# Another order of the seven products of an output projection, and lo parts of eleven weight tiles formed by transfers that add

## The chip, the cores and the metric

The kernel runs on one core of one Trainium2 chip. The metric is the device time of one execution in microseconds. Before the change it is 800.76 us, the median of three runs (800.46 to 800.78).

## The reference: what is computed

One decoder layer on 512 tokens of width 1024, all in float32. Three mixers work side by side on the normalised input (attention in a sliding window with sinks, stick-breaking attention, attention to a memory of 256 entries); their outputs are gated, added, projected and normalised. A gated feed-forward network (FFN) of inner width 2816 follows:

```python
u = rms_norm(h, ln_mix_pre[l])
proj = jnp.einsum('bsd,de->bse', u, w_in[l])
...
merged = (g[:, :, 0] * jnp.einsum('bse,ed->bsd', y_swa, w_branch_swa[l])
          + g[:, :, 1] * jnp.einsum('bse,ed->bsd', y_sb, w_branch_sb[l])
          + g[:, :, 2] * jnp.einsum('bse,ed->bsd', y_mem, w_branch_mem[l]))
mix = jnp.einsum('bsd,de->bse', merged, w_out[l])
h = h + rms_norm(mix, ln_mix_post[l])
u = rms_norm(h, ln_ffn_pre[l])
a = jax.nn.silu(jnp.einsum('bsd,df->bsf', u, w_gate[l])) * jnp.einsum('bsd,df->bsf', u, w_up[l])
ffn = jnp.einsum('bsf,fd->bsd', a, w_down[l])
h = h + rms_norm(ffn, ln_ffn_post[l])
```

The change lies between `merged` and the first products with `w_gate` and `w_up`.

## The kernel before, in words

**Splitting.** TensorE multiplies rounded values (the type fp32r in the profile). To keep float32 accuracy each operand is split into hi, the rounded value, and lo, the rest. `split` does this with two instructions: ScalarE (ACT) casts raw to hi (L135), VectorE (DVE) subtracts hi from raw to get lo (L136). A product of two split operands takes three matmuls, hi with hi, lo with hi and hi with lo (`mm3`, L169, L171, L172). The second reads lo of the left operand, the tokens, the third lo of the right one, the weights.

**Seven products.** The larger matrix products are taken as 2 x 2 blocks with seven block products in place of eight, named p1 to p7. That needs sums of weight blocks and sums of token blocks. Sums of weights are made mostly by transfers: a plain load brings one block into SBUF (SyncE, called SP, issues it), and a transfer on the queue of GpSimd (POOL) adds another block from memory onto the same tile (`accum_op=ALU.add`). In the output projection that is `wo_raw` and `wo_plus` (L1034; tiles of 128x512, 256 KB), in the FFN `g_raw` (L1233) and `g_plus` (L1236; tiles of 128x1024, 512 KB). A tile that needs two or three additions gets them one after the other, each waiting for the landing of the one before. The blocks of p1, p2 and p4 of the FFN are plain blocks of the weights, and so are those of p2 and p3 of the output projection.

**Output projection.** `mix_mm(p, i)` is one block product for half i of the tokens: four k tiles times three matmuls of 512 columns, 12 matmuls, summed in a PSUM bank x, y or w. Products with the same bank add up in it: p1, p6, p7, p4 in x, p5, p3 in y, p2 in w. Between the products a join copies the state of a bank or combines it with an earlier copy: ACT after p1, p5 and p6, DVE after p2, p3 (mkp, L1113) and p7. A product may only add to its bank once the join has read the state before. `wo_split` makes hi and lo of the weight tiles.

**Normalising and turning.** `mix(t)` normalises 128 token rows (t from 0 to 3), adds the residual and normalises again for the FFN: two squares and the short steps of the inverse root on ACT (t_m, r_m), long products on DVE; it ends in the tile mt. Tiles 0 and 1 are ready after p3 of half 0 and half 1, tiles 2 and 3 after p4 of half 0 and half 1. `turn(t)` transposes the rows of a tile on TensorE (L1177, eight transposes of 128x128 into two PSUM banks `ut`), and `place` splits them into the left operands of the FFN: B11 and B21 from tiles 0 and 1 (casts at L1165), T1 and others from tiles 2 and 3.

**FFN.** The object `fs` of class `Stream` holds a list of units, each one weight tile of 128x1024 with its 24 matmuls of 256 columns. The list begins

```python
seq = [("p1", 0), ("p2", 0), ("p1", 1), ("p1", 2), ("p2", 1), ("p2", 2)]
seq += [("p5", 0), ("p6", 0), ("p5", 1), ("p3", 0), ("p6", 1), ("p7", 0), ("p3", 1), ("p7", 1), ("p4", 0)]
```

with (product, chunk). The text counts units from 0, so unit 1 is p2 of chunk 0, unit 2 p1 of chunk 1 and unit 3 p1 of chunk 2. In the profile p1 sums in gx, p2 in gw, later ones in gy. `fs.ahead(l, s)` issues the loads up to unit l and the splits up to unit s; `load_at(i, ...)` hangs further loads and additions on unit i: the plain loads for p5, p6 and p3 of chunk 0 on unit 2, their six additions on unit 3 (one for p5, two for p6, three for p3), the tile "t" for p7 of chunk 0 with its addition on unit 4.

**What sets the order.** A scheduler puts the instructions on the engines' queues largely as the program writes them, with pieces under `tc.high_priority()` pulled forward. Each engine then works its queue strictly in order: an instruction that waits holds up all behind it, and that holds for the transfers that SP and POOL issue too. `first.close()` ends the life of a pool of tiles (`wp`), and the pool `fp` of the FFN tiles takes its memory. The `hi`, `lo` and `raw` tiles of `fp` so wait for the last reader of the old ones, which is p3 of half 1, for its weights lie in `wp`.

The change lies between 380 and 490 us of 798. The functions that it touches and what calls them:

Of the kernel before, what the change touches and what calls it, by code (L numbers as in the profile page):

```python
# [32 lines left out]
class Stream:  # L33
# [24 lines left out]
    def ahead(self, load_to, split_to):  # L58
        while self.loaded <= min(load_to, len(self.units) - 1):
            u = self.units[self.loaded]  # L60
            for fn in u["load"]:
                fn()
            u["raw"] = u["src"]() if callable(u["src"]) else self.load(u["src"], u["n"])
            self.loaded += 1
        while self.have <= min(split_to, len(self.units) - 1):
            u = self.units[self.have]
            for fn in u["split"]:
                fn()
            u["hl"] = self.split(u["raw"], u["n"])
            self.have += 1  # L70

    def later(self, us, fn):
# [31 lines left out]
def tile_kernel(ctx, tc, a):  # L104
# [27 lines left out]
    def split(raw, hi, lo, sign=1.0):  # L132

        if sign == 1.0:
            ins = nc.scalar.copy(hi, raw)  # L135
            lows = nc.vector.tensor_tensor(lo, raw, hi.bitcast(F32), op=ALU.subtract)  # L136
        else:
            ins = nc.scalar.mul(hi, raw, sign)
            lows = nc.vector.scalar_tensor_tensor(lo, raw, sign, hi.bitcast(F32), op0=ALU.mult, op1=ALU.subtract)
        if "behind" in st:  # L140
            after(ins, st["behind"][0])
            after(lows, st["behind"][1])
        return ins

    uid = [0]

# [889 lines left out]
    def wo_split(p, key, k):  # L1036
        if p not in ("p6", "p3"):
            hl = tuple(ck(f"wo{p}{x}{k}", F32R)[:, :] for x in "hl")
        else:
            if k % 2 == 0:  # L1040
                uid[0] += 1
                st["wo_two"] = [wp.tile([P, 1024], F32R, tag=x, name=f"{x}{uid[0]}", bufs=4) for x in ("hi", "lo")]
            hl = tuple(x[:, (k % 2) * 512 : (k % 2) * 512 + 512] for x in st["wo_two"])
        split(wsum[key][k][:, :], *hl)
        wt[(p, k)] = hl

    def rstd_small(name, ss):
# [37 lines left out]
    def turned_d(k):  # L1085
        split(merged[k][:, 256:], *(x[:, 256:] for x in mrd[k]))
# [3 lines left out]
    def mix_mm(p, i):  # L1090
        if p in ("p1", "p5", "p2"):
            mbank[(MIX[p], i)] = aps(f"m{MIX[p]}{i}")
        ps = mbank[(MIX[p], i)]
        for k in range(4):
            if p == "p1":
                x, o = ma[k // 2], (k % 2) * 256
            else:
                x, o = {"p2": (mbd, 0), "p4": (mbd, 256), "p5": (mqs, 256), "p3": (mqs, 0), "p6": (mrd, 0), "p7": (mrd, 256)}[p]
                x = x[k]
            mm3(ps[:, :], cols(x, o + i * P, P), wt[(p, k)], k == 0 and p in ("p1", "p5", "p2"), k == 3)  # L1100
        with tc.high_priority():
            if p in ("p1", "p5", "p6"):
                t = mkeep[(p, i)] = ck(f"mk{p}{i}")
                nc.scalar.copy(t[:, :], ps[:, :])
            elif p == "p2":
                t = mkeep[("p1", i)]
                nc.vector.tensor_tensor(t[:, :], ps[:, :], t[:, :], op=ALU.add)
            elif p == "p3":
                t = mkeep[("p6", i)]
                nc.vector.tensor_tensor(t[:, :], ps[:, :], t[:, :], op=ALU.subtract)  # L1110
            elif p == "p7":
                t = mkeep[("p5", i)]
                nc.vector.tensor_tensor(t[:, :], t[:, :], ps[:, :], op=ALU.subtract)  # L1113

    def mix(t):
        xr = hres[t]
        i = t % 2
        ps = (mkeep[("p1", i)], mkeep[("p6", i)]) if t < 2 else (mbank[("x", i)], mkeep[("p5", i)])
        ss, ss2 = small(f"ssm{t}", 2), small(f"ssh{t}", 2)
        tmp = [ck(f"mt{t}{h}") for h in range(2)]  # L1120
        for h in (1, 0):
            nc.scalar.activation(tmp[h][:, :], ps[h][:, :], AF.Square, accum_out=ss[:, h : h + 1])
        for h in (1, 0):
            nc.vector.tensor_tensor(tmp[h][:, :], ps[h][:, :], gpost[h][:, :], op=ALU.mult)
        r = rstd_small(f"m{t}", ss)
        for h in range(2):
            nc.vector.scalar_tensor_tensor(xr[h][:, :], tmp[h][:, :], r, xr[h][:, :], op0=ALU.mult, op1=ALU.add)
            nc.scalar.activation(tmp[h][:, :], xr[h][:, :], AF.Square, accum_out=ss2[:, h : h + 1])
        r2 = rstd_small(f"h{t}", ss2)
        for h in range(2):  # L1130
            st["mixed"] = nc.vector.scalar_tensor_tensor(
                tmp[h][:, :], xr[h][:, :], r2, gfpre[h][:, :], op0=ALU.mult, op1=ALU.mult
            )
        return tmp
# [38 lines left out]
    def turn(t, tmp):  # L1173
        pt = [aps(f"ut{t}{h}") for h in range(2)]
        for h in range(2):
            for k in range(4):
                nc.tensor.transpose(pt[h][:, k * P : (k + 1) * P], tmp[h][:, k * P : (k + 1) * P], ident[:, :])  # L1177
        turned[t] = pt
        if t < 2:
            turned[t] = [ck(f"ur{t}{h}") for h in range(2)]  # L1180
            for h in range(2):
                place(("B11", "B21")[h], t, pt[h])
                nc.scalar.copy(turned[t][h][:, :], pt[h][:, :])
            return
        t1 = ck(f"t1{t}")
        nc.vector.tensor_tensor(t1[:, :], pt[0][:, :], turned[t - 2][0][:, :], op=ALU.subtract)
        st[("t1", t)] = t1
        return place("T1", t, t1)
# [38 lines left out]
    def g_src(n, i, j):  # L1227
        return a["w_gu"][:, n + i * HF, j].rearrange("p g k n -> p (g k n)")
# [285 lines left out]
    for k in range(4):  # L1514
        wo_split("p7", "b", k)
        turned_d(k)
    mix_mm("p3", 0)
    table("natural_log_exp_and_others")
    tmp[0] = mix(0)
    for k in range(4):  # L1520
        wo_split("p4", "r", k)
    for p in ("p5", "p6", "p3"):
        mix_mm(p, 1)
    first.close()
    fp = ctx.enter_context(tc.tile_pool(name="fp", bufs=9, reuse_waits="tile"))

    def f_split(raw, n):
        uid[0] += 1
        hi = fp.tile([P, 1024], F32R, tag="hi", name=f"hi{uid[0]}", bufs=4)
        lo = fp.tile([P, 1024], F32R, tag="lo", name=f"lo{uid[0]}", bufs=4)  # L1530
        if isinstance(raw, list):
            for i, x in enumerate(raw):
                split(x[:, :], hi[:, i * 512 : (i + 1) * 512], lo[:, i * 512 : (i + 1) * 512])
        else:
            split(raw[:, :n], hi[:, :n], lo[:, :n])
        return hi, lo

    fs = Stream(None, f_split, LOAD_AHEAD + 1)
# [43 lines left out]
        with tc.high_priority():  # L1582
            tmp[t] = mix(t)

    fs.ahead(2, -1)
    mixed(1)
    mix_mm("p7", 0)
    turn(0, tmp[0])
    mix_mm("p4", 0)
    mixed(2)  # L1590
    fs.ahead(4, 1)
    mix_mm("p7", 1)
    mix_mm("p4", 1)
    turn(1, tmp[1])
    mixed(3)
# [116 lines left out]
```

## Time and profile before

| | |
|---|---|
| median of three runs | 800.76 us (800.46 to 800.78) |
| the profiled execution | 800.18 us |
| its span, first to last instruction | 798.4 us |
| mean granted TensorE clock | 0.995 |
| instructions in the span | 12825 |
| chain that ended last | PE 93%, DVE 4%, ACT 1%, issue 1% |
| transfers | 120.70 MB, mean 151 GB/s |
| POOL's additions of FFN tiles (L1236) | 27 of 512 KB, median 7.4 us to landing |
| SP's plain loads of FFN tiles | 57 of 512 KB, median 5.6 us to landing |

Times in the profile are counted from the first instruction of the span. PE is TensorE's matmul, PEld its loading of weights, SPq the queue of SP. Of a group of instructions the profile gives line, engine, operation, and the tiles it writes and reads (out<-in); "x4" is a count, and three durations such as 603/618/632 are the shortest, the median and the longest in ns. In a list of waits "PE mx L169 <- DVE t_m L1055: 0.9, 1, 0.9" says that matmuls of line 169 into mx waited 0.9 us in all, once, at most 0.9, until DVE's instruction for t_m ended. In a timeline the columns are start, duration, engine, line, operation and tiles; brackets at the end hold the idle time before it and what ended it, and a row with x3 stands for three instructions in a run. A PE row's duration is longer than the distance to the next start, since matmuls are pipelined. In a list of transfers the last number is the us from issue to landing, a median where there are several.

### The profile page before, as it was taken

What the parts mean: (1) busy time and instruction counts of PE and PEld (TensorE: products, weight loads), DVE (VectorE), ACT (ScalarE), POOL (GpSimd) and SP (SyncE); (2) the same over time, 40 slices, a digit from 0 to 9 for tenths busy, and PEclk for the clock granted to TensorE, in tenths of its full rate; (3) what the DMA queues carried; (4) which work ended last, traced back from release to release, by engine and by line L of the source; (5) the groups of instructions that cost most, each with busy time, mean ns of one, the idle gap of its engine ahead of it and who ended that gap; (6) DMA issues with size and microseconds to landing.
All of it is one profiled execution on the core that took longest, in us unless ns stands there. A gap on an engine that the chain in (4) does not pass through costs nothing.

```text
span 798.4 us, 12825 instructions
## 1 busy us (share of the span) xinstructions
PE 782.0 (98%) x4851; PEld 694.0 (87%) x4851; DVE 637.1 (80%) x1010; ACT 467.7 (59%) x868; POOL 94.0 (12%) x119
## 2 busy tenths in 40 slices
PE   9999999999999999999999889999999999999996
PEld 6899887877878899899887689999999999888885
DVE  6998976854778795986798889967677767898797
ACT  6566755644654555666655767545444444666573
POOL 0102100000000001000161120100100000205200
PEclk9999999999999999999999999999999999999998
DMA  8443356122243208238675897987777752859802
GB/s 302 134 149 106 118 166 205 53 82 76 80 102 79 59 27 238 52 88 258 183 137 154 252 222 195 280 230 201 184 182 182 187 157 67 197 126 225 205 0 106
DMA packets 44750, 120.70 MB, mean 151 GB/s; under 512 B 4976, under 2 KB 6912, under 8 KB 44688
## 3 DMA queue, kind: packets, MB, share of 16 engines
q1 hardware_dynamic: 32448, 86.66, 33.3%
q0 software_dynamic: 11952, 33.02, 22.6%
q8 instruction: 38, 0.62, 0.3%
q14 instruction: 24, 0.20, 0.1%
q10 hardware_dynamic: 288, 0.20, 0.1%
HBM read 116.19 MB, written 3.67 MB: 150 GB/s over the span
## 4 chain that ended last, share of the span: by engine, by line
PE 93%; DVE 4%; ACT 1%; issue 1%; DVEq 0%; ACTq 0%
PE gx L169 5%; PE gx L172 5%; PE gx L171 5%; PE g L169 3%; PE g L172 3%; PE br L169 3%; PE br L171 3%; PE g L171 3%; PE br L172 3%; PE gy L169 3%; PE gy L172 3%; PE gy L171 3%; PE x L172 3%; PE x L169 3%; PE x L171 2%; PE qx L169 1%
## 5 line engine op out<-in xcount | busy, mean ns | idle before, releaser
L135 ACT CAST hi<-gw 128x1024 fp32r<-128x1024 f32 x77 | 80.0, 1048 | 76.6 <-DVE gw L1254 36.0
L136 DVE TENSOR_TENSOR lo<-gw,hi 128x1024 fp32r<-128x1024 f32 x77 | 93.5, 1222 | 34.0 <-ACT hi L135 34.0
L135 ACT CAST hi<-raw 128x1024 fp32r<-128x1024 f32 (+2 forms) x52 | 53.8, 1040 | 51.0 <-PE g L171 13.8
L136 DVE TENSOR_TENSOR lo<-raw,hi 128x1024 fp32r<-128x1024 f32 (+2 forms) x52 | 62.8, 1213 | 18.0 <-ACT hi L135 17.8
L1236 POOL DMA_DIRECT2D gw<-in_w_gu x27 | 23.3, 900 | 191.7 <-DMA gw<-in_w_gu 112.4
L135 ACT CAST hi<-r 128x1024 fp32r<-128x1024 f32 (+1 forms) x24 | 23.6, 982 | 19.1 <-PE y L172 5.3
L171 PE MATMUL x<-lo,lh 128*128 128x512 f32 x88 | 34.2, 389 | 0.0
L169 PE MATMUL x<-hi,lh 128*128 128x512 f32 x88 | 34.2, 389 | 0.0
L172 PE MATMUL x<-hi,ll 128*128 128x512 f32 x88 | 34.1, 389 | 0.0
L832 DVE TENSOR_TENSOR_SCAN p<-r,anew 128x512 f32<-128x512 f32 (+1 forms) x24 | 24.7, 1040 | 8.1 <-ACT r L189 7.6
L136 DVE TENSOR_TENSOR lo<-r,hi 128x1024 fp32r<-128x1024 f32 (+1 forms) x24 | 27.1, 1130 | 3.1 <-ACT hi L135 3.1
L136 DVE TENSOR_TENSOR lo<-qw,hi 128x1024 fp32r<-128x1024 f32 x18 | 22.0, 1220 | 8.1 <-ACT hi L135 8.1
L135 ACT CAST hi<-qw 128x1024 fp32r<-128x1024 f32 x18 | 18.9, 1050 | 16.1 <-PE g L171 3.7
L136 DVE TENSOR_TENSOR lo<-bp,hi 128x512 fp32r<-128x512 f32 x33 | 22.7, 720 | 6.3 <-ACT hi L135 6.2
L135 ACT CAST hi<-bp 128x512 fp32r<-128x512 f32 x33 | 19.1, 619 | 13.6 <-DMA bp<-in_w_dn 5.2
L169 PE MATMUL gw<-B21h,hi 128*128 128x256 f32 x88 | 25.4, 289 | 0.8 <-ACT B21h L1165 0.8
L172 PE MATMUL gy<-T1h,lo 128*128 128x256 f32 x88 | 25.0, 284 | 0.8 <-DVE lo L136 0.8
L169 PE MATMUL gx<-B11h,hi 128*128 128x256 f32 x88 | 25.4, 289 | 0.0
L172 PE MATMUL gw<-B21h,lo 128*128 128x256 f32 x88 | 25.3, 287 | 0.0
L171 PE MATMUL gx<-B11l,hi 128*128 128x256 f32 x88 | 25.2, 286 | 0.0
L172 PE MATMUL gx<-B11h,lo 128*128 128x256 f32 x88 | 25.2, 286 | 0.0
L171 PE MATMUL gw<-B21l,hi 128*128 128x256 f32 x88 | 25.2, 286 | 0.0
(1020 smaller groups left out, 2946.8 us busy)
## 6 DMA issues: line engine op xcount, KB each, us to landing
gw<-in_w_gu SPq DMA_DIRECT2D x57, 512.0 KB, 5.6
gw<-in_w_gu POOLq DMA_DIRECT2D x27, 512.0 KB, 7.4
raw<-in_w_p SPq DMA_DIRECT2D x26, 512.0 KB, 4.0
qw<-in_w_p SPq DMA_DIRECT2D x15, 512.0 KB, 4.0
raw<-in_w_br SPq DMA_DIRECT2D x12, 512.0 KB, 3.7
bp<-in_w_dn SPq DMA_DIRECT2D x22, 256.0 KB, 8.4
r<-in_w_dn POOLq DMA_DIRECT2D x10, 512.0 KB, 8.4
qw<-in_w_p POOLq DMA_DIRECT2D x6, 512.0 KB, 7.8
```

Of the source, the lines that this page charges most:

```text
L135: ins = nc.scalar.copy(hi, raw)
L136: lows = nc.vector.tensor_tensor(lo, raw, hi.bitcast(F32), op=ALU.subtract)
L169: one = nc.tensor.matmul(out, lh, rh, start=start, stop=False, skip_group_check=True)
L171: nc.tensor.matmul(out, *two, start=False, stop=False, skip_group_check=True)
L172: st["product"] = nc.tensor.matmul(out, *three, start=False, stop=stop, skip_group_check=True)
L832: ins = nc.vector.tensor_tensor_scan(p[:, :w], left1[i][:, :w], anew[:, o : o + w], 0.0, op0=ALU.mult, op1=ALU.max)
L1236: nc.gpsimd.dma_start(gw[(n, key)][:, :], g_src(n, i, j), accum_op=ALU.add)
```

## The change

**Lo by a transfer.** A new function `split_dma` takes the place of `split` for eleven plain weight tiles. ACT casts raw to hi as before, then ACT writes minus hi into lo, and POOL issues a transfer that adds the same block from memory once more onto lo. DVE's subtraction falls away. Eight of the tiles belong to p2 and p3 of the output projection, three are FFN units 1, 2 and 3.

**Order of the products.** From p7's splits on the program goes, with the half in brackets: p5(1), p3(0), mix(0) now at high priority, p6(1), p7(0), p3(1), end of the pool, mixed(1), loads to unit 3 with the split of unit 0, p4(0), mixed(2), p7(1), turn(0), loads to unit 4 with the splits of units 1 to 3, p4(1), turn(1), mixed(3). Before it was p3(0), mix(0), p5(1), p6(1), p3(1), end of the pool, loads to unit 2, mixed(1), p7(0), turn(0), p4(0), mixed(2), loads to unit 4 with the splits of units 0 and 1, p7(1), p4(1), turn(1), mixed(3), then the splits of units 2 and 3.

```diff
-            u["hl"] = self.split(u["raw"], u["n"])
+            u["hl"] = u.get("way", self.split)(u["raw"], u["n"])
...
+    def split_dma(raw, hi, lo, src):
+
+        nc.scalar.copy(hi, raw)
+        nc.scalar.mul(lo, hi.bitcast(F32), -1.0)
+        nc.gpsimd.dma_start(lo, src, accum_op=ALU.add)
...
-        split(wsum[key][k][:, :], *hl)
+        if p in ("p2", "p3"):
+            j, h = (1, 0) if p == "p2" else (1, 1)
+            split_dma(wsum[key][k][:, :], *hl, a["w_out"][:, h, 4 * j + k])
+        else:
+            split(wsum[key][k][:, :], *hl)
...
+    mix_mm("p5", 1)
     mix_mm("p3", 0)
     table("natural_log_exp_and_others")
-    tmp[0] = mix(0)
+    with tc.high_priority():
+        tmp[0] = mix(0)
     for k in range(4):
         wo_split("p4", "r", k)
-    for p in ("p5", "p6", "p3"):
-        mix_mm(p, 1)
+    for p, i in (("p6", 1), ("p7", 0), ("p3", 1)):
+        mix_mm(p, i)
     first.close()
...
+    def f_split_dma(raw, src):
+        uid[0] += 1
+        hi = fp.tile([P, 1024], F32R, tag="hi", name=f"hi{uid[0]}", bufs=4)
+        lo = fp.tile([P, 1024], F32R, tag="lo", name=f"lo{uid[0]}", bufs=4)
+        split_dma(raw[:, :], hi[:, :], lo[:, :], src)
         return hi, lo
...
-    fs.ahead(2, -1)
     mixed(1)
-    mix_mm("p7", 0)
-    turn(0, tmp[0])
+    for i, (p, n) in enumerate(seq[:4]):
+        if i > 0:
+            fs.units[i]["way"] = lambda raw, w, n=n, j=(0 if p == "p1" else 1): f_split_dma(raw, g_src(n, 0, j))
+    fs.ahead(3, 0)
     mix_mm("p4", 0)
     mixed(2)
-    fs.ahead(4, 1)
     mix_mm("p7", 1)
+    turn(0, tmp[0])
+    fs.ahead(4, 3)
     mix_mm("p4", 1)
     turn(1, tmp[1])
     mixed(3)
```

The rows that follow are the engines' queues around the change. A name ends in the tile's number, which differs between the two kernels; in brackets stand the semaphores that an instruction waits for (DMAHW are landings of plain loads, DMASW landings of POOL's transfers). The lines of `mm3` are 169, 171 and 172 before and 175, 177 and 178 now.

TensorE at the end of p7 of half 0 (wop7, wop4 and hi/lo are weights of p7, p4 and p3, mx and my the banks), before:

```order
L172 MATMUL mx_4418<-wop7h_4607,mrl_4483 128x512
L169 MATMUL mx_4418<-wop4h_4661,mbd4h 128x512 [waits DVE_49,Activation_49]
L171 MATMUL mx_4418<-wop4l_4662,mbd4h 128x512
L172 MATMUL mx_4418<-wop4h_4661,mbd4l 128x512
L169 MATMUL my_4677<-hi_4318,mqh_4448 128x512 [waits Activation_49]
```

and now:

```order
L178 MATMUL mx_4426<-wop7h_4615,mrl_4491 128x512
L175 MATMUL my_4621<-hi_4322,mqh_4456 128x512 [waits Activation_49]
L177 MATMUL my_4621<-lo_4323,mqh_4456 128x512
...
L178 MATMUL my_4621<-hi_4347,mql_4469 128x512
L175 MATMUL mx_4426<-wop4h_4684,mbd4h 128x512 [waits DVE_49,Activation_49]
```

Where p4 of half 0, which waits for the join after p7, stood directly behind p7 with three of its matmuls ahead of p3 of half 1, all 12 matmuls of p3 of half 1 now stand between the two.

POOL's queue behind the additions of the output projection; gw are raw FFN tiles (4728, 4730 and 4732 those of p5, p6 and p3 of chunk 0, 4859 that of p7 of chunk 0, 4862 one of chunk 1), before:

```order
L1236 DMA gw_4728<-in_w_gu 128x1024 [waits DMAHW1_49,PE_49]
L1236 DMA gw_4730<-in_w_gu 128x1024 [waits DMAHW2_49,DMASW7_49,PE_49]
L1236 DMA gw_4732<-in_w_gu 128x1024 [waits DMAHW3_49,DMASW0_49,PE_49]
L1236 DMA gw_4730<-in_w_gu 128x1024 [waits DMASW7_49,DMASW1_49]
L1236 DMA gw_4732<-in_w_gu 128x1024 [waits DMASW2_49,DMASW0_49]
L1236 DMA gw_4859<-in_w_gu 128x1024 [waits DMAHW6_49,DMASW3_49]
L1236 DMA gw_4862<-in_w_gu 128x1024 [waits DMAHW7_49,DMASW4_49]
L1236 DMA gw_4732<-in_w_gu 128x1024 [waits DMASW5_49,DMASW2_49]
```

and now, where 4783, 4785, 4787, 4884 and 4887 are the same five in the same order, and lo_4892, lo_4897 and lo_4902 belong to units 1, 2 and 3:

```order
L1246 DMA gw_4783<-in_w_gu 128x1024 [waits DMAHW1_49,PE_49]
L149 DMA lo_4892<-in_w_gu 128x1024 [waits DMASW7_49,Activation_49]
L1246 DMA gw_4785<-in_w_gu 128x1024 [waits DMAHW2_49,DMASW0_49,PE_49]
L1246 DMA gw_4787<-in_w_gu 128x1024 [waits DMAHW3_49,DMASW1_49,PE_49]
L1246 DMA gw_4785<-in_w_gu 128x1024 [waits DMASW2_49,DMASW0_49]
L1246 DMA gw_4884<-in_w_gu 128x1024 [waits DMAHW6_49,DMASW3_49]
L1246 DMA gw_4787<-in_w_gu 128x1024 [waits DMASW4_49,DMASW1_49]
L149 DMA lo_4897<-in_w_gu 128x1024 [waits DMASW5_49,Activation_49]
L149 DMA lo_4902<-in_w_gu 128x1024 [waits DMASW6_49,Activation_49]
L1246 DMA gw_4787<-in_w_gu 128x1024 [waits DMASW7_49,DMASW4_49]
L1246 DMA gw_4887<-in_w_gu 128x1024 [waits DMAHW7_49]
```

The transfer for lo of unit 1 stands second, and those for units 2 and 3 stand eighth and ninth, behind the second additions to 4785 and 4787; on TensorE the third matmul of unit 2 (gx from B11h_3613 and lo_4897) now waits for that transfer.

ACT where it places the first turned rows (ut_4899 and ut_4900 are tile 1 turned, hi_4957 and hi_4961 units 2 and 3), before:

```order
L1165 CAST B11h_3613<-ut_4899 128x2x128 [waits PE_49]
L135 CAST hi_4957<-gw_4734 128x1024 [waits DMAHW4_49]
L1165 CAST B21h_3617<-ut_4900 128x2x128 [waits PE_49]
L189 ACTIVATE t_m_4827<-ssm_4817,b_m_4825 128x1 [waits DVE_49,Activation_49]
L135 CAST hi_4961<-gw_4857 128x1024 [waits DMAHW5_49]
L189 ACTIVATE r_m_4828<-t_m_4827 128x1 [waits Activation_49]
L1165 CAST B11h_3615<-ut_4899 128x2x128 [waits DVE_49]
L1165 CAST B21h_3619<-ut_4900 128x2x128 [waits DVE_49]
```

and now (ut_4862 is tile 0, ut_4918 tile 1, hi_4896/lo_4897 and hi_4901/lo_4902 units 2 and 3; the last row shown is the second quarter of tile 1):

```order
L1175 CAST B11h_3613<-ut_4918 128x2x128 [waits PE_49]
L147 CAST hi_4896<-gw_4789 128x1024 [waits DMAHW4_49]
...
L148 ACTIVATE lo_4897<-hi_4896 128x1024 [waits Activation_49]
...
L1175 CAST B11h_3615<-ut_4862 128x2x128 [waits DVE_49]
L147 CAST hi_4901<-gw_4797 128x1024 [waits DMAHW5_49]
L1193 COPY ur_4872<-ut_4862 128x512 [waits DVE_49]
L1138 ACTIVATE mt_4817,ssh_4816<-xr_4504 128x512 [waits DVE_49]
L1138 ACTIVATE mt_4818,ssh_4816<-xr_4505 128x512 [waits DVE_49]
L1175 CAST B21h_3617<-ut_4863 128x2x128
...
L148 ACTIVATE lo_4902<-hi_4901 128x1024
...
L1175 CAST B11h_3615<-ut_4918 128x2x128
```

Between the first and the second cast of tile 1 into B11 there now lie the rest of tile 0's casts, two casts and two multiplications of 128x1024, a copy, and two squares for the normalisation.

More of the change, by code (lines that the diff above doesn't have):

```diff
@@ L1535, in f_split @@
             split(raw[:, :n], hi[:, :n], lo[:, :n])
+        return hi, lo
+    def f_split_dma(raw, src):
[3 more added lines that the diff above has]
+        split_dma(raw[:, :], hi[:, :], lo[:, :], src)
         return hi, lo
```

## The prediction, made before the changed kernel had run

> **What bounds the kernel now.** I read the page first, then the waits, the table of windows, and the timelines of TensorE and of POOL between 430 and 490 us, where the change lies. Every line number in this part is that of the kernel before.
>
> ```profile
> PE 782.0 (98%) x4851; PEld 694.0 (87%) x4851; DVE 637.1 (80%) x1010; ACT 467.7 (59%) x868; POOL 94.0 (12%) x119
> ```
>
> TensorE is busy for 98% of the span, so a thing costs or gains time only where TensorE stands still. The windows say where that is (columns: length, then busy us of PE, PEld, DVE, ACT, POOL, granted PE clock, DMA share, GB/s):
>
> ```profile
> 410.00:420.00 10.00, 10.00 (x46) 8.27 (x45) 10.00 (x23) 6.67 (x17) 3.89 (x4) 1.00 0.70 149
> 430.00:440.00 10.00, 9.13 (x41) 7.27 (x40) 7.58 (x16) 5.25 (x14) 0.00 (x0) 1.00 0.03 6
> 440.00:450.00 10.00, 9.22 (x44) 6.98 (x43) 8.43 (x20) 7.04 (x18) 1.44 (x2) 1.00 0.66 243
> 450.00:460.00 10.00, 6.97 (x36) 5.79 (x35) 9.38 (x24) 8.53 (x23) 1.14 (x2) 0.83 1.04 282
> 460.00:470.00 10.00, 7.74 (x64) 7.30 (x62) 8.15 (x22) 6.46 (x20) 3.49 (x4) 1.00 1.03 244
> ```
>
> Up to 437 us TensorE is full. In 430 to 470 it is idle for 0.87 + 0.78 + 3.03 + 2.26 = 6.9 us, and in 450 to 470 the DMA engines are full (1.04, 1.03). The waits of TensorE name the causes:
>
> ```profile
> PE ut L1177 <- DVE mt L1131: 4.5, 3, 2.2
> PE mx L169 <- DVE t_m L1055: 0.9, 1, 0.9
> PE gw L169 <- ACT B21h L1165: 0.8, 1, 0.8
> PE mx L169 <- DVE mkp L1113: 0.8, 1, 0.8
> PE gy L172 <- DVE lo L136: 0.8, 1, 0.8
> PE gy L169 <- ACT hi L135: 0.2, 1, 0.2
> ```
>
> Two waits for joins of the output projection (mx, 0.9 and 0.8), three for the normalised rows that the transposes read (ut, 4.5 in all), and little else. No wait for a transfer is among them. POOL's own timeline shows transfers that are slow all the same, with nobody on TensorE behind them:
>
> ```profile
> 448.10 0.86 POOL L1236 DMA_DIRECT2D gw<-in_w_gu  x1 [23.57 <-DMA gw<-in_w_gu]
> 449.42 0.86 POOL L1236 DMA_DIRECT2D gw<-in_w_gu  x1 [0.46 <-issue]
> 450.70 0.86 POOL L1236 DMA_DIRECT2D gw<-in_w_gu  x1 [0.42 <-issue]
> 462.73 0.86 POOL L1236 DMA_DIRECT2D gw<-in_w_gu  x1 [11.17 <-DMA gw<-in_w_gu]
> 466.29 2.63 POOL L1236 DMA_DIRECT2D gw<-in_w_gu  x3 [2.70 <-DMA gw<-in_w_gu]
> 472.03 0.86 POOL L1236 DMA_DIRECT2D gw<-in_w_gu  x1 [3.11 <-DMA gw<-in_w_gu]
> ```
>
> These are the transfers that add, onto the raw tiles of FFN products p5, p6 and p3. The fourth stands 11.17 us in the queue until the landing of an earlier one, since a second addition to the same tile waits for the first. The list of issues in three windows, each around one of the first three and then the fourth and the last, gives their times to landing:
>
> ```profile
> gw<-in_w_gu POOLq DMA_DIRECT2D x1, 512.0 KB, 10.3
> gw<-in_w_gu POOLq DMA_DIRECT2D x1, 512.0 KB, 12.8
> gw<-in_w_gu POOLq DMA_DIRECT2D x1, 512.0 KB, 15.3
> gw<-in_w_gu POOLq DMA_DIRECT2D x1, 512.0 KB, 6.5
> gw<-in_w_gu POOLq DMA_DIRECT2D x1, 512.0 KB, 9.2
> ```
>
> So they land at 448.10 + 10.3 = 458.4, 462.2, 466.0, 469.2 and 481.2 us. While plain loads run beside them they land 3.8 us apart. After that they are alone: the five from 466.0 to 481.2 (fourth to eighth) lie 15.2/5 = 3.04 us apart, the shortest known step being 472.0 - 469.2 = 2.8, the longest 3.2.
>
> **The change, part by part.** First, the order of the products. Before, p4 of half 0 comes right behind p7 of half 0 and waits for its join:
>
> ```profile
> 437.43 0.39 PE L172 MATMUL mx<-wop7h,mrl 128*128 128x512 f32 x1
> 438.69 0.47 PE L169 MATMUL mx<-wop4h,mbd4h 128*128 128x512 f32 x1 [0.87 <-DVE t_m L1055]
> 439.46 0.40 PE L169 MATMUL my<-hi,mqh 128*128 128x512 f32 x1
> ```
>
> Now p3 of half 1 stands between, 12 matmuls at the 0.227 us that starts lie apart in a product (438.69 would have been 437.66). p3 of half 1 so starts at 437.66 rather than 439.46: 1.8 us earlier. The second wait for a join (0.8) gets the 8 transposes of rows 0 to 127 as cover. Both are gone: worth 1.03 + 0.8, and with p3's join 1.8 earlier, the normalisation of tile 1 comes up to 1.8 us earlier to its 2.2 us wait. That would be 3.6 us, if nothing later held TensorE.
>
> What else hangs on p3 of half 1 are the loads of the FFN weights. The queue of SP says so, and when they go out:
>
> ```profile
> SPq L1233 <- PE my L172: 20.9, 1, 20.9
> 442.41 2.97 SPq L1233 DMA_DIRECT2D gw<-in_w_gu  x6
> ```
>
> They start 1.8 us earlier too: 440.6.
>
> Second, the eight w_out tiles of p2 and p3. DVE loses eight subtractions of 0.68, ACT gets eight multiplications, for which the row shows the casts of the same size (0.62 us), POOL eight issues of 0.9 us:
>
> ```profile
> L136 DVE TENSOR_TENSOR lo<-wob,hi x4: 677/679/1487, 401.6 to 407.2; 128x512 fp32r<-128x512 f32 x4
> L135 ACT CAST wop2h<-wob x4: 603/618/632, 387.4 to 395.5; 128x512 fp32r<-128x512 f32 x4
> L1034 POOL DMA_DIRECT2D wor<-in_w_out x12: 850/858/1193, 374.2 to 423.7; - x12
> DMA to landing us min/median/max: 4.3/7.1/9.2
> ```
>
> The last cast for p2 is at 395.5; two ACT steps, seven issues ahead of the last one on POOL (7 x 0.9) and the longest landing (9.2) make 412.3, and the first of those tiles is read at about 416, that of p3 at about 430. TensorE has no gap there to gain. I cost this part at nothing; its cover is four microseconds, and past it each microsecond is one.
>
> Third, the three FFN tiles: the lo parts of units 1, 2 and 3 (p2 of chunk 0, p1 of chunks 1 and 2). This decides. On DVE one took 1.22 us:
>
> ```profile
> L136 DVE TENSOR_TENSOR lo<-gw,hi 128x1024 fp32r<-128x1024 f32 x77 | 93.5, 1222 | 34.0 <-ACT hi L135 34.0
> L135 ACT CAST hi<-gw 128x1024 fp32r<-128x1024 f32 x77 | 80.0, 1048 | 76.6 <-DVE gw L1254 36.0
> ```
>
> Now it is 1.05 on ACT (a multiplication of the size of that cast) and a 512 KB addition on POOL's queue, in the window with the full DMA engines. By the order of POOL shown ahead, lo of unit 1 stands second, but those of units 2 and 3 stand eighth and ninth: behind the second additions to gw_4785 and gw_4787, each of which waits for the first to land. That is where 11.17 and 2.70 us were waited before. And TensorE reads lo of unit 2 with the third matmul of that unit, which before ran at
>
> ```profile
> 466.10 0.29 PE L172 MATMUL gx<-B11h,lo 128*128 128x256 f32 x1
> 470.05 1.23 PE L1177 MATMUL ut<-c_ident,mt 128*128 128x128 f32 x8 [1.15 <-DVE mt L1131]
> ```
>
> The sum. The first group of additions now has four in it (gw_4783, lo of unit 1, gw_4785, gw_4787) and ended before at 466.0 with three. It starts 1.8 earlier and is one addition longer: 466.0 - 1.8 + 3.0 = 467.2. Only then POOL can issue the second addition to gw_4787 and, 0.86 later, lo of unit 2 (468.2 or so). In the queue of transfers that one is fourth after 467.2 (the second addition to gw_4785, gw_4884, the second to gw_4787, lo): 467.2 + 4 x 3.04 = 479.4 us. Lo of unit 3 lands at 482.4. Against 466.10 the third matmul of unit 2 comes 13.4 us later, at 479.5.
>
> Ahead of that TensorE has nothing else to do for about ten microseconds, and its clock will drop. Before, after the idle stretch that began at 452, matmuls with 256 columns started 0.21 apart and not 0.12:
>
> ```profile
> 458.28 0.41 PE L172 MATMUL gw<-B21h,lo 128*128 128x256 f32 x1
> 458.50 0.41 PE L169 MATMUL gw<-B21h,hi 128*128 128x256 f32 x1
> 466.34 0.28 PE L171 MATMUL gx<-B11l,hi 128*128 128x256 f32 x1
> 466.46 0.28 PE L172 MATMUL gx<-B11h,lo 128*128 128x256 f32 x1
> ```
>
> The clock of 0.83 over 10 us is 3.4 us at half. So 16 matmuls at 0.212 and the remaining six at 0.12, together 4.1 us instead of 2.64, and the transposes of tile 3 start at 483.6, where they started at 470.05 (their own wait of 1.15 is then long over): 13.5 us later. Lo of unit 3 is there by its third matmul at about 485. Two later waits, 0.8 and 0.2 for gy, fall away, since DVE and ACT get ahead meanwhile: 12.5 us remain. What the first part gains is swallowed, since it lies ahead of a wait for a transfer. The profiled execution took 800.18 us around its span of 798.4, and the median is 800.76, 0.58 above it: 810.9 for the span, 812.7 for such an execution, **813.3** for the median.
>
> Bounds: if the added addition fits into gaps and the steps are 2.8, lo of unit 2 lands at 464.2 + 11.2 = 475.4, and with a full clock 7.1 us remain: 807.9. If it costs 3.8, the steps are 3.2, all 22 matmuls run slowly and no later wait falls away, it is 468.0 + 12.8 = 480.8 and 15.5 us: 816.3. I take the middle steps, as they come from five transfers of this very queue and size.
>
> The rows above have 6.5 to 15.3 us from issue to landing. The Trainium skill ("DMA: Bandwidth & Descriptors", the section "Anatomy of one DMA — SWDGE (gpsimd) path") fits such a transfer as 2.0 us plus its bytes over 436e3. My estimate from that page for 524288 bytes is 3.2 us, and by it no addition would wait long for another and lo of unit 2 would be there before 460: by that rule the second rival below would happen. The trace disagrees in all five rows, since the engines are full.
>
> **The rivals.** *The transfers are in time, but turning is late.* The second additions would have to be issued before 458. Then TensorE waits for the turned rows: between the casts of tile 1's first quarter (about 452) and of its second (B11h_3615), ACT now has four steps of 1.05, two squares, a copy and small ones, some 8 us, with DVE's two products for tile 2 (0.7 each) behind them, against 3.4 us from first to last cast before. Unit 0 goes on at about 462.8, and the transposes of tile 3 come at about 472.2, 2.1 late, less the 1.0: 801.9. For it speaks that DVE has three long steps less; against it the 11.17 us.
>
> *Faster: the cover works.* The mechanism is the first part alone: joins hidden (1.03 + 0.8), tile 1 earlier (1.8). 800.76 - 3.6 = 797.2. It decides only if lo of unit 2 lands before 466 and the casts of turned rows keep their old places; for it speak the waits of TensorE quoted first, against it both orders.
>
> *The w_out additions are late as well.* Sixteen additions of 256 KB, at half of 3.04 each, take 24 us from 389 to 413 on DMA engines that were at 0.70 in 410 to 420 already. If ACT stands in its order behind a cast of a tile not landed, mbd7h comes after 416 and p2 waits; at 3 us: 816.3.
>
> **How the numbers follow.** The queue as computed: 0.78. Late w_out additions on top: 0.08. In time with late turning: 0.08. Faster: 0.06. The likeliest case alone is 807.9 to 816.3; I stretch it to **805 to 817**, since a landing some microseconds earlier is the easiest miss, and leave the two cases below 803 outside. About 0.2% (1.6 us) can be told from no change: faster 0.06, same 0.05 (most of the late turning), slower 0.89.
>
> **What would show it.** A wait of TensorE for a transfer into lo, 8 to 11 us, at the third matmul of p1 of chunk 1, with a PE clock below 1 after it; POOL issuing that transfer only at about 468, behind a long wait for gw; no more waits for t_m or mkp, and loads from about 440.6. I am wrong if lo of unit 2 is issued before 460 or lands less than 6 us after issue, or if TensorE stops ahead of 437.

## The result: 1.7% slower

| | before | changed |
|---|---|---|
| median | 800.72 us (800.46 to 800.78, 4 runs) | 813.97 us (813.38 to 814.44, 4 runs) |
| ratio | | 1.0166 (95% interval 1.0148 to 1.0183) |
| profiled execution, span | 800.18, 798.4 us | 813.38, 811.6 us |
| mean granted TensorE clock | 0.995 | 0.984 |

813.3 us was forecast, 805 to 817 the range. First the page of the changed kernel, busy time and chain:

```profile
PE 784.5 (97%) x4851; PEld 697.1 (86%) x4851; DVE 630.6 (78%) x999; ACT 474.9 (59%) x879; POOL 103.4 (13%) x130
PE 90%; DVE 3%; issue 3%; DMA 2%; POOL 1%; ACT 0%; SPq 0%; DVEq 0%; POOLq 0%; ACTq 0%
```

Transfers and POOL, which had no share in the chain that ended last, have one now. The waits of TensorE say which:

```profile
PE gx L178 <- DMA lo<-in_w_gu: 10.7, 1, 10.7
PE gx L175 <- ACT B11h L1175: 3.9, 1, 3.9
PE ut L1187 <- DVE mt L1141: 2.6, 2, 1.3
PE mw L175 <- ACT mbd7h L135: 0.7, 1, 0.7
```

One wait of 10.7 us for a transfer into lo, where no wait for a transfer was before. The two waits for joins (mx) are gone, and those for ut are 2.6 in place of 4.5 us. Two larger waits are new beside it: 3.9 us for the second quarter of the turned rows, and 0.7 us in p2 of the output projection, far ahead of the rest. The same stretches as before the change:

```profile
410.00:420.00 10.00, 9.13 (x40) 6.93 (x39) 8.67 (x17) 5.12 (x10) 6.68 (x6) 1.00 1.06 205
430.00:440.00 10.00, 10.00 (x46) 8.29 (x45) 7.87 (x17) 7.40 (x18) 0.00 (x0) 1.00 0.03 6
440.00:450.00 10.00, 10.00 (x49) 8.23 (x48) 9.16 (x22) 6.64 (x15) 1.50 (x3) 1.00 0.63 229
450.00:460.00 10.00, 5.04 (x23) 3.84 (x21) 7.38 (x22) 9.34 (x26) 2.02 (x3) 0.76 1.05 296
470.00:480.00 10.00, 0.00 (x0) 0.00 (x0) 5.45 (x12) 4.90 (x10) 3.94 (x5) 0.61 1.06 205
480.00:490.00 10.00, 9.38 (x59) 9.38 (x60) 3.19 (x5) 2.62 (x5) 0.12 (x1) 0.71 0.69 135
```

Between 430 and 450 TensorE is now full, so the covers work. From 470 to 480 it does nothing at all, while the DMA engines are full (1.06). The queue of POOL and the chain of waits around the end of that stretch:

```profile
448.50 0.86 POOL L1246 DMA_DIRECT2D gw<-in_w_gu  x1 [23.77 <-PE mx L178]
449.25 1.00 POOL L149 DMA_DIRECT2D lo<-in_w_gu  x1
449.82 2.21 POOL L1246 DMA_DIRECT2D gw<-in_w_gu  x2
466.37 1.75 POOL L1246 DMA_DIRECT2D gw<-in_w_gu  x2 [14.34 <-DMA gw<-in_w_gu]
469.68 0.86 POOL L1246 DMA_DIRECT2D gw<-in_w_gu  x1 [1.56 <-DMA gw<-in_w_gu]
470.21 2.09 POOL L149 DMA_DIRECT2D lo<-in_w_gu  x2
```

```profile
470.21 10.36 DMA lo<-in_w_gu
480.62 0.58 PE gx L178
```

The transfer for lo of unit 2 goes out at 470.21 us, behind second additions that waited 14.34 and 1.56 us for landings, and lands 10.4 us later. ACT had written minus hi for it long before:

```profile
455.41 1.04 ACT L148 ACTIVATE lo<-hi 128x1024 fp32r<-128x1024 f32 x1
```

That ended at 456.45, so the transfer stood ready for 13.8 us. What follows the wait runs slowly:

```profile
480.62 0.58 PE L178 MATMUL gx<-B11h,lo 128*128 128x256 f32 x1 [10.67 <-DMA lo<-in_w_gu]
485.27 0.41 PE L178 MATMUL gx<-B11h,lo 128*128 128x256 f32 x1
485.48 1.24 PE L1187 MATMUL ut<-c_ident,mt 128*128 128x128 f32 x8
```

The 22 matmuls from 480.62 to 485.48 take 0.22 us each and not 0.12. The transposes of tile 3 start at 485.48 instead of 470.05: 15.4 us late. 2.2 of these come back within the next 35 us, where TensorE had waited 0.8 and 0.2 us for gy and some shorter times more, since DVE and ACT had got ahead; the span is 13.2 us longer.

### The profile page after: what moved, and what is told of

Same layout as the page of the kernel before. It is cut to its first block, busy times and chain, and to the rows that moved or that the text cites. A ratio compares the mean times of both kernels' runs of the same rounds, so it can differ in the third digit from the quotient of the medians.

```text
span 811.6 us, 12844 instructions
## 1 busy us (share of the span) xinstructions
PE 784.5 (97%) x4851; PEld 697.1 (86%) x4851; DVE 630.6 (78%) x999; ACT 474.9 (59%) x879; POOL 103.4 (13%) x130
## 4 chain that ended last, share of the span: by engine, by line
PE 90%; DVE 3%; issue 3%; DMA 2%; POOL 1%; ACT 0%; SPq 0%; DVEq 0%; POOLq 0%; ACTq 0%
PE gx L178 5%; PE gx L175 5%; PE gx L177 5%; PE g L175 3%; PE g L178 3%; PE br L177 3%; PE br L175 3%; PE g L177 3%; PE br L178 3%; PE gy L178 3%; PE gy L177 3%; PE gy L175 3%; PE x L175 2%; PE x L178 2%; PE x L177 2%
## 5 line engine op out<-in xcount | busy, mean ns | idle before, releaser
L135 ACT CAST hi<-gw 128x1024 fp32r<-128x1024 f32 x74 | 77.0, 1050 | 76.5 <-DVE gw L1264 36.0
L136 DVE TENSOR_TENSOR lo<-gw,hi 128x1024 fp32r<-128x1024 f32 x74 | 89.9, 1224 | 33.9 <-ACT hi L135 33.9
L178 PE MATMUL gx<-B11h,lo 128*128 128x256 f32 x88 | 26.8, 304 | 10.7 <-DMA lo<-in_w_gu 10.7
L178 PEld LDWEIGHTS gx<-B11h,lo 128*128 128x128 f32 x88 | 18.6, 212 | 10.9 <-DMA lo<-in_w_gu 10.9
L178 PE MATMUL gy<-N22h,lo 128*128 128x256 f32 x88 | 25.0, 284 | 0.0
L175 PE MATMUL gx<-T4h,hi 128*128 128x256 f32 x88 | 25.0, 284 | 0.0
```

The source lines that it names most:

```text
L175: one = nc.tensor.matmul(out, lh, rh, start=start, stop=False, skip_group_check=True)
L178: st["product"] = nc.tensor.matmul(out, *three, start=False, stop=stop, skip_group_check=True)
```

## The experiments

### One part at a time, and the place in the queue

**The order alone.** All eleven lo parts by DVE again; the edit is in two conditions:

```diff
-        if p in ("p2", "p3"):
+        if p in ():
...
-        if i > 0:
+        if False:
```

> The new order of the seven products alone: all eleven lo parts are again made by DVE's subtraction. If the loss comes from the FFN transfers that add (the theory), the 10.7 us wait for lo is gone, the 2.2 us that TensorE lost around p2 is gone too, and what stays is the hidden joins (1.6 us gained) against a late second quarter of turned rows (about 2 us of the 3.9, since ACT has two of its four long steps less): 800 us, 798.5 to 801.5. If the order itself carries the loss (first rival), 805 us or more. If the late turned rows cost nothing, 797.

Measured: 800.53 us, ratio 0.9993 (0.9984 to 1.0002). The order neither gains nor loses. Its waits show why:

```profile
PE ut L1187 <- DVE mt L1141: 3.1, 2, 2.3
PE gw L175 <- ACT B21h L1175: 1.8, 1, 1.8
PE gx L177 <- DVE B11l L1176: 1.5, 1, 1.5
PE mx L175 <- DVE mkp L1123: 0.3, 1, 0.3
```

The waits for joins shrink from 1.7 to 0.3 us, and the later two waits for ut (1.16 and 1.15) are gone; 3.3 us of waits for placed rows (B21h, B11l) have come in their stead, where 0.8 was before.

**The w_out tiles, without the FFN tiles** (only the second of the two conditions changed):

> The new order with the eight w_out tiles by transfers that add, the three FFN tiles by DVE's subtraction. Theory: no wait for lo, but TensorE again waits in p2 for mbd7 (0.7 + 0.2 us and the late start behind it, 2.2 in all): 802 us, 800.5 to 803.5, about 2 above the order alone. Rival, that this part costs nothing: as the order alone.

Measured: 803.02 us, 1.0028 (1.0017 to 1.0039), 2.5 us above the order alone. This part was not free.

**The FFN tiles, without the w_out tiles** (only the first condition changed):

> The new order with the three FFN tiles by transfers that add, the w_out tiles by DVE's subtraction. Theory: the wait for lo of unit 2 stays at 10 to 11 us; what is gained ahead of it (2.2 us in p2) also moves the FFN loads and with them all landings 2.2 us forward: 811.8 us, 810.5 to 813.5. If what lies ahead of the wait is swallowed entirely (the landings stay): 814. If the w_out additions made the wait: below 805.

Measured: 810.75 us, 1.0115 (1.0101 to 1.0129). The rows (waits, then POOL's timeline and TensorE's):

```profile
PE gx L178 <- DMA lo<-in_w_gu: 7.8, 1, 7.8
PE gx L175 <- ACT B11h L1175: 3.9, 1, 3.9
```

```profile
467.88 0.86 POOL L1246 DMA_DIRECT2D gw<-in_w_gu  x1 [1.91 <-DMA gw<-in_w_gu]
468.42 2.10 POOL L149 DMA_DIRECT2D lo<-in_w_gu  x2
```

```profile
477.80 0.58 PE L178 MATMUL gx<-B11h,lo 128*128 128x256 f32 x1 [7.79 <-DMA lo<-in_w_gu]
```

The three FFN tiles by themselves cost 10.2 us against the order alone, and the whole mechanism is there without the w_out tiles. The loads start at 441.19 instead of 442.82 us, and lo of unit 2 arrives 2.8 us earlier (477.80 and 480.62): a delay ahead of the pool's end is handed on to the landings behind it.

**The same transfers in another order on POOL.** The changed kernel with an order-only edge that puts the lo transfers of units 2 and 3 ahead of the second additions; those hang on unit 5 instead of 3 and 4, so that the edge points backwards:

```diff
-        nc.gpsimd.dma_start(lo, src, accum_op=ALU.add)
+        st["lo_dma"] = nc.gpsimd.dma_start(lo, src, accum_op=ALU.add)
...
-        nc.gpsimd.dma_start(gw[(n, key)][:, :], g_src(n, i, j), accum_op=ALU.add)
+        ins = nc.gpsimd.dma_start(gw[(n, key)][:, :], g_src(n, i, j), accum_op=ALU.add)
+        if n > 0 or i == 0:
+            after(ins, st["lo_dma"])
...
+    for key, i, j in (("p6", 0, 0), ("p3", 0, 0), ("p3", 0, 1), ("t", 0, 0)):
+        load_at(5, g_plus, 0, key, i, j)
```

> The changed kernel with one thing moved: on POOL's queue the transfers for lo of units 2 and 3 stand ahead of the second additions to the raw tiles of p6 and p3 and of the addition for p7. Traffic and instructions are the same. Theory (place in an in-order queue): lo of unit 2 goes out at about 457 instead of 470 us, stands fifth in the queue of transfers and lands about 2.9 us after the fourth, which landed at 469.6: 472.5 instead of 480.6. TensorE stands still for about 4 us instead of 10.7 and the time is 806 us, 804 to 808. Rival (the extra traffic in full DMA engines is the cause, wherever the transfers stand): 812 to 814.

Measured: 803.18 us, 1.0032 (1.0014 to 1.0050). POOL's timeline, then waits of TensorE, then its row:

```profile
456.55 0.86 POOL L149 DMA_DIRECT2D lo<-in_w_gu  x1 [4.95 <-ACT r_m L195]
460.96 0.86 POOL L149 DMA_DIRECT2D lo<-in_w_gu  x1 [3.55 <-ACT r_h L195]
465.90 0.86 POOL L1246 DMA_DIRECT2D gw<-in_w_gu  x1 [4.08 <-DMA gw<-in_w_gu]
```

```profile
PE gx L175 <- ACT B11h L1175: 4.7, 1, 4.7
PE gx L178 <- DMA lo<-in_w_gu: 1.1, 1, 1.1
```

```profile
471.61 0.39 PE L178 MATMUL gx<-B11h,lo 128*128 128x256 f32 x1 [1.07 <-DMA lo<-in_w_gu]
```

The same eleven added transfers, 10.8 us less time. Lo of unit 2 goes out at 456.55 and lands at about 471.5, close to the 472.5 expected, and the wait falls from 10.7 to 1.1 us. So the place in the queue makes 10.8 of the 13.2 us, and not the traffic. My expectation of 806 was 3 too high: I had allowed for a wait of about 4 us, but TensorE asks for lo only at 470.5 (471.61 - 1.07), and the 22 matmuls behind the short wait run fast (2.74 us, last section).

### What the w_out tiles cost, and where

The rows of the changed kernel, TensorE in p2 and ACT ahead of it:

```profile
418.89 0.50 PE L175 MATMUL mw<-wop2h,mbd7h 128*128 128x512 f32 x1 [0.65 <-ACT mbd7h L135]
439.86 0.39 PE L175 MATMUL my<-hi,mqh 128*128 128x512 f32 x1
```

```profile
407.90 0.62 ACT L135 CAST hi<-wor 128x512 fp32r<-128x512 f32 x1 [3.70 <-DMA wor<-in_w_out]
411.10 0.62 ACT L135 CAST hi<-wor 128x512 fp32r<-128x512 f32 x1 [2.58 <-DMA wor<-in_w_out]
418.21 0.62 ACT L135 CAST mbd7h<-g 128x512 fp32r<-128x512 f32 x1 [1.33 <-DVE g L607]
```

ACT stood before the casts of p6's weight tiles, whose additions had not landed, and the cast of mbd7, further back in the same queue, came at 418.21 (414.87 before). What this cast waited for last was DVE's g (1.33 us), and DVE had been stopped by the first of the late casts:

```profile
408.55 0.94 DVE L136 TENSOR_TENSOR lo<-wor,hi 128x512 fp32r<-128x512 f32 x1 [2.51 <-ACT hi L135]
```

So the late landings can reach p2 through ACT and through DVE behind it.

**Only p2's four tiles by transfers** (the FFN tiles by DVE):

```diff
-        if p in ("p2", "p3"):
+        if p == "p2":
```

> The new order; lo by a transfer that adds for the four w_out tiles of p2 alone (those of p3 and the three FFN tiles by DVE's subtraction). In the run with all eight, ACT stood 3.7 and 2.6 us in its queue before the casts of p6's tiles, because their additions (issued from 400 us) shared the DMA engines with the lo additions of p3 (issued 398 to 406). Theory (those landings, seen through ACT's in-order queue, are what p2 waits for): the four of p2 go out before 399 and are nearly all landed, the wait for mbd7 is gone, 800.5 to 801.5 us, as the order alone. Rival (each added transfer or each multiplication on ACT costs its share): half of the 2.5 us, 801.8, with a wait for mbd7 left.

Measured: 801.93 us, 1.0011 (0.9996 to 1.0026), single runs from 800.33 to 805.25. Its profile has no wait for mbd7, as the theory says, yet the median lies where the rival puts it, and the interval includes 1. It does not decide between them.

**All eight, but those of p3 behind p6's additions on POOL** (the FFN tiles by DVE; `st["late"]` marks the tiles of p3, `st["plus"]` is the latest addition of `wo_plus`):

```diff
-        nc.gpsimd.dma_start(lo, src, accum_op=ALU.add)
+        ins = nc.gpsimd.dma_start(lo, src, accum_op=ALU.add)
+        if st.get("late"):
+            after(ins, st["plus"])
```

> The new order with the eight w_out tiles by transfers that add, the three FFN tiles by DVE's subtraction, and one thing moved: on POOL's queue the four lo additions of p3 stand behind the four second additions to the tiles of p6. Traffic and instructions are those of the run that lost 2.5 us against the order alone. Theory (ACT stands in its in-order queue before the casts of p6's tiles, whose additions land late beside the lo additions of p3): the idle stretches of 3.7 and 2.6 us of ACT before those casts go, no wait for mbd7, 800.5 to 801.5 us. Rival (the traffic or the eight multiplications on ACT as such): 802.5 to 803.5.

Measured: 800.85 us, 1.0005 (0.9996 to 1.0013): 0.3 us above the order alone in place of 2.5, with the same transfers and multiplications. The idle stretches of ACT, which I had expected to vanish with it, only became shorter (4.49 and 1.86 us in the run with all eight in their old places):

```profile
407.36 0.62 ACT L135 CAST hi<-wor 128x512 fp32r<-128x512 f32 x1 [3.06 <-DMA wor<-in_w_out]
409.90 0.62 ACT L135 CAST hi<-wor 128x512 fp32r<-128x512 f32 x1 [1.92 <-DMA wor<-in_w_out]
```

TensorE waits 0.2 us for mbd7 there, where that run has 0.8. That the order of these transfers on POOL carries most of the cost is shown by the medians (2.2 us apart). The two profiled executions are only 0.9 us apart (801.96 and 801.10), so the traces do not show all of it, and how much went through ACT's queue is not separated.

### Attempts to be faster than the kernel before

The order alone moved waits from one place to another. Five further edits, all with lo by DVE, asked whether any of them can be taken out.

**Transposes of tiles 2 and 3 one unit later**, in the kernel before:

```diff
-    go(1)
+    go(2)
     turn(2, tmp[2])
-    go(3)
+    go(4)
     behind(*turn(3, tmp[3]))
     fs.hold = 5
-    go(4)
     turn_n2(2)
     behind(*turn_n2(3))
```

> The kernel before with one edit: the transposes of tiles 2 and 3 stand one FFN unit later in the program, so that TensorE does not wait for their rows (1.16 and 1.15 us before). If nothing behind needs the turned rows earlier: 798.5 us, 797.9 to 799.3. If the rows are then late for p5 (unit 6), new waits for T1 of about the same size: 800.5 to 801.

Measured: 803.64 us, 1.0033 (1.0020 to 1.0047).

```profile
478.96 1.99 ACT L135 CAST hi<-gw 128x1024 fp32r<-128x1024 f32 x2
480.06 0.58 PE L169 MATMUL gw<-B21h,hi 128*128 128x256 f32 x1 [3.58 <-ACT hi L135]
```

The waits for the rows of tiles 2 and 3 (1.16 and 1.15 us before) shrink to 0.45 us, but one of 3.58 us for hi is new. It is that of unit 5 (p2 of chunk 2), for the 24 matmuls of unit 4 start at 472.30 and lie ahead of it. The last lines of the edit show why. Before, `go(4)` had unit 5 split ahead of `turn_n2`, which makes the N2 operands from tiles 2 and 3. Now that call is gone, and the split comes behind `turn_n2(3)`: ACT casts N2h from 477.74 and hi of unit 5 at 478.96, where it cast it at 475.15 in the kernel before. So the loss of 3.0 us does not show that later transposes cannot gain; a run with unit 5 split in its old place was not made.

**p3 of half 1 ahead of p7 of both halves**, in the new order, with the same shift of the transposes (not shown again):

```diff
-    for p, i in (("p6", 1), ("p7", 0), ("p3", 1)):
+    for p, i in (("p6", 1), ("p3", 1)):
         mix_mm(p, i)
...
-    fs.ahead(3, 0)
+    fs.ahead(2, -1)
...
+    mix_mm("p7", 0)
+    mix_mm("p7", 1)
     mix_mm("p4", 0)
     mixed(2)
-    mix_mm("p7", 1)
     turn(0, tmp[0])
-    fs.ahead(4, 3)
+    fs.ahead(4, 1)
```

> The new order with plain splits, but p3 of half 1 ahead of p7 of both halves, and the transposes of tiles 2 and 3 one unit later. p3 of half 1 then ends 12 matmuls, 2.7 us, earlier than in the order alone, so the rows of tile 1 are no longer waited for 2.3 us; the waits of 1.8 and 1.5 us for the placed rows stay in part, since ACT still has two squares of tile 2 between them. 797 us, 795.5 to 799. If the chain of tile 1 is held by other things on DVE and ACT (rival): 799.5 to 801.

Measured: 804.37 us, 1.0042 (1.0026 to 1.0057). Its waits, and two rows of DVE:

```profile
PE ut L1187 <- DVE mt L1141: 5.9, 1, 5.9
PE gw L175 <- ACT hi L135: 3.6, 1, 3.6
```

```profile
449.70 1.22 DVE L136 TENSOR_TENSOR lo<-gw,hi 128x1024 fp32r<-128x1024 f32 x1
451.51 1.22 DVE L136 TENSOR_TENSOR lo<-gw,hi 128x1024 fp32r<-128x1024 f32 x1 [0.25 <-ACT hi L135]
```

The rows of tile 1 came no earlier (transposes from 455.60, from 452.97 and 454.89 with the order alone) although p3 of half 1 started 3.1 us earlier (435.02, not 438.09), so the wait for them grew. Splits of FFN units, the two rows shown, and products of tile 2 stand between the steps of tile 1 on DVE. Apart from that the run carries the loss of the edit above, the late cast of unit 5.

**The same with the normalisation of tile 2 behind the turning of tile 1** (`mixed(2)` moved behind `turn(1, tmp[1])`, which is under high priority):

> As the run before, with the normalisation of tile 2 standing behind the turning and placing of tiles 0 and 1 in the program, so that no squares of tile 2 lie between the casts of tile 1. Theory (the squares and products of tile 2 are what delays the second quarter): no wait for B11 or B21 above 1 us, 795.5 us, 794.5 to 797. Rival (the rows of tile 2 then come late and their transposes stop TensorE by as much): 797 to 799.

Measured: 806.34 us, 1.0068 (1.0049 to 1.0087). The rival's side, and worse: the waits for B11 and B21 are gone, but the rows of tile 1 come at 455.27, only 0.3 us earlier (a wait of 5.29), and those of tile 2 are late now (2.01 and 1.30 us).

**Splits of units 2 and 3 behind the placing of tile 1**, in the kernel before (`turn` returns its last cast and subtraction):

```diff
-    turn(1, tmp[1])
+    last = turn(1, tmp[1])
     mixed(3)
+    behind(*last)
     fs.ahead(5, 3)
```

> The kernel before with one edit: the splits of FFN units 2 and 3 stand behind the placing of tile 1 on ACT and DVE. Two casts of 1.05 us that lay between the four casts of tile 1's placing come after it. The wait for B21 (0.8 us) should go, the four casts come closer together, and the transposes of tile 2 come as before: 800 us, 799.3 to 800.8. If the lo of unit 2 is then late for TensorE at 466: 801 to 802.

Measured: 800.92 us, 1.0002 (0.9994 to 1.0011). The wait for B21 fell from 0.8 to 0.3 us, as expected, and nothing of it is left at the end.

**Unit 4 split early, as a cover for the transposes**, on top of that and of the shifted transposes:

```diff
     go(1)
+    saved = st.pop("behind")
+    fs.ahead(6, 4)
+    st["behind"] = saved
+    go(2)
     turn(2, tmp[2])
-    go(3)
+    go(4)
...
```

> As the run before, and FFN unit 4 is split right after unit 0, free of the order behind the normalisation of tile 3, with the transposes of tile 2 after unit 1 and of tile 3 after unit 3: unit 4 can then run while TensorE would wait for the rows of tiles 2 and 3 (1.16 and 1.15 us before). The edit that moved the transposes alone lost 3 us to a wait of 3.6 us for hi of unit 4. Theory (that wait came from the split's place behind tile 3): the wait is gone, 798 us, 797 to 799.5. If the chain of normalising tiles 2 and 3 on DVE and ACT is the bound whatever stands in between: 800 to 801.5, with waits for T1.

Measured: 807.71 us, 1.0091 (1.0077 to 1.0105). Waits for hi are 6.9 us now, in two parts: 2.40 us for unit 4 at 466.45 and 4.48 for unit 5 at 485.01. The wait of 3.6 us that the edit was to remove had been that of unit 5, whose cast stands behind `turn_n2(3)` here too. The first part has its cause in a row of ACT:

```profile
465.35 1.04 ACT L135 CAST hi<-gw 128x1024 fp32r<-128x1024 f32 x1 [2.99 <-DMA gw<-in_w_gu]
```

The early cast waits 2.99 us for its load, in the middle of the normalisation of tile 2, and everything behind it on ACT waits too. It is the fault of the change under study once more, on another queue. No version found beats the kernel before, but four of the five carry the late cast of unit 5 (waits of 3.58, 3.58, 1.71 and 4.48 us), so they leave open what the ideas would give without it.

## Why the prediction was right, by its own steps

**The step that decides, lo of unit 2 behind the second additions:** right, and shown by the two runs that undo it: making the three FFN lo parts by DVE takes 11.0 us off (813.97 to 803.02), the other place in the queue 10.8. Forecast and trace: POOL issues at about 468, measured 470.21; TensorE waits 8 to 11 us, measured 10.67; third matmul of unit 2 at 479.5, measured 480.62; transposes of tile 3 at 483.6, measured 485.48. In the run with the FFN tiles alone, where nothing ahead disturbs, the first addition to p3 lands at about 467.9 (467.2 forecast).

**The step of 3.04 us** between additions that are alone: from 469.68 to 480.6 four of them landed, 2.7 us apart on average, just below the lower bound of 2.8. That took 1.2 us off what the later start (469.68, not 467.2) added.

**"I cost this part at nothing"** (the w_out tiles): wrong. It cost 2.5 us alone. In the changed kernel p3 of half 1 began at 439.86, not at 437.66, and the loads at 442.82, not at 440.6; without those tiles the loads start at 441.19, so 1.6 of these 2.2 us are theirs. The gain of 1.8 us in the landings did not come. The cover of four microseconds was reckoned for the landings of the w_out tiles themselves. What was late were other tiles' additions on the same DMA engines, and the casts queued behind them. The third rival named this, with 3 us and a chance of 0.08; its mechanism happened beside the likeliest case, with 1.6 us in the trace and 2.5 by itself. The sign that I gave for being wrong, a stop of TensorE ahead of 437, was seen (418.89), and the total held all the same.

**"In time with late turning"**, the first rival, was right as a mechanism too. The casts of the second quarter on ACT:

```profile
456.45 0.36 ACT L1175 CAST B11h<-ut 128x256 fp32r<-128x256 f32 x1
456.70 1.05 ACT L147 CAST hi<-gw 128x1024 fp32r<-128x1024 f32 x1
458.12 0.65 ACT L1138 ACTIVATE mt<-xr 128x512 f32<-128x512 f32 x1
459.81 1.06 ACT L148 ACTIVATE lo<-hi 128x1024 fp32r<-128x1024 f32 x1
461.10 0.40 ACT L1175 CAST B11h<-ut 128x256 fp32r<-128x256 f32 x1
```

The row at 456.45 follows the multiplication for lo of unit 2; then a cast, squares of tile 2 and the multiplication for unit 3 stand ahead of tile 1's B11h at 461.10, for which TensorE waits 3.9 us. In the changed kernel this stands inside the longer wait for lo and costs nothing of its own. With lo in time it is what remains: that rival's 801.9 us for it stand against 803.18 measured, which hold the w_out tiles as well. The sum of the decisive step rightly took no term for it.

**The clock:** forecast 16 slow matmuls and 4.1 us for the 22, from a stretch of 3.4 us at half clock as before the change; all 22 were slow, 4.86 us, for this stretch was four times as long (last section). **What comes back:** 1.0 us was forecast, 2.2 came. The third matmul was 1.1 us later than forecast, the clock cost 0.8 more, and 1.2 more came back: 12.5 + 1.1 + 0.8 - 1.2 = 13.2. That 813.3 stands so near to 813.97 is partly owed to terms that cancel.

**The first part**, 3.6 us "if nothing later held TensorE": by itself (the order alone) it gave a ratio of 0.9993, not distinguishable from 1. The joins were hidden as reckoned (1.7 to 0.3 us); the third gain, tile 1 earlier, did not come, since the rows of tile 1 are held by DVE and ACT and not by p3: with p3 3.1 us earlier still they came no earlier.

## What to carry to other kernels

A transfer that takes work off a busy engine becomes an entry of an in-order queue: before counting what it saves, read what stands ahead of it there and what that waits for, and give the entry with the nearest reader the front place (10.8 us here, with the same traffic). Where DVE and ACT carry chains that end in TensorE's operands, moving a product or a transpose can merely move the wait, as the order alone did here. Look first at which chain would be late next, and at what an edit puts behind other work unasked: four of the five attempts lost time to one cast that had slipped behind another step. A cast whose load has not landed holds up all work behind it, so issuing it early is no safe default.

## What the runs showed of the hardware

Idle time of TensorE can have a second price. After the wait of 10.67 us 22 matmuls took 4.86 us; after the wait of 1.07 us, with the other place in the queue, the same 22 took 474.35 - 471.61 = 2.74 us:

```profile
474.35 1.04 PE L1187 MATMUL ut<-c_ident,mt 128*128 128x128 f32 x8
```

The granted clock in these traces is either full or half, and the stretches at half in this part are multiples of 3.41 us: 3.41 before the change (456.1 to 459.5), 10.24 and 13.65 in the changed kernel (455.2 to 465.4 and 472.2 to 485.9), 6.83 with the other place in the queue (460.2 to 467.0). The long ones begin 2.3 us into the wait of 10.67 and 3.6 us into a wait of 4.73 us for B11h (456.62 to 461.35). The one at 455.2 begins behind waits of only 1.31 and 1.27 us, with eight transposes between and after them; behind waits of 1.27 and 1.26 us in the other run the clock stayed full.

The Trainium skill ("TensorE: Matmul & The Clock Gate", section "HAM oscillation — how this bites in real kernels") says that gaps over some 3.4 us bring half the clock. The waits of 10.67, 4.73 and 1.07 us agree with that; the stretch that begins at 455.2 does not follow from any single gap of that length. The Trainium skill lets the full clock return about 4 us into steady work (same page, "What you observe"). Here it returned 5.3 us after the end of the wait of 10.67 and 5.7 after that of 4.73, and 3.9 us after the wait of 3.93 us for B11h in the changed kernel, so the page's figure is met once and exceeded twice.

Four additions of 512 KB in a row landed 2.7 us apart on average (469.68 to 480.6), and one that had three others ahead of it took 10.4 us from issue to landing, with the DMA engines full (1.06).
